# Two-layer hybrid mixer on one core: pacing of the second norm, both first weight splits in one projection job, and scan projections by segments

## Chip, cores and metric

One core of one Trainium2 chip. The metric is the device time of one execution in microseconds (us), the median of several runs. All inputs and outputs are float32; the projections run on TensorE (PE in the rows) as three passes of rounded parts, as told below.

## What is computed

Two layers over 512 latent tokens and 256 context tokens of width 1024. Each layer normalises the tokens, projects them (`w_in`), runs three mixers beside one another (windowed attention, a gated linear scan called GLA, a retention scan), merges them, projects again (`w_out`), adds the result to the stream, normalises a second time and runs a gated MLP with a width-3 convolution, whose down projection is added to the stream. The second layer computes the latent tokens alone from its queries on.

```python
h = rms_norm(x, norm1_g[l]) * (1.0 + sc1) + sh1
hc = rms_norm(ctx, norm1_g[l]) * (1.0 + csc1) + csh1
y, yc = token_mixers(h, hc, w_in[l], ...)
x = x + gt1 * y
h2 = rms_norm(x, norm2_g[l]) * (1.0 + sc2) + sh2
x = x + gt2 * conv_ffn(h2, ffn_up[l], ffn_conv_w[l], ffn_conv_b[l], ffn_down[l])
if with_ctx:
    ctx = ctx + cgt1 * yc
    ...

def rms_norm(a, g):
    af = a.astype(F32)
    y = af * lax.rsqrt(jnp.mean(af * af, axis=-1, keepdims=True) + EPS)
    return (y * g.astype(F32)).astype(a.dtype)
```

## The kernel before

Tokens lie along the free axis (768 columns: 512 latent, 256 context), channels on the partitions, 8 blocks of 128. A projection is a list of **jobs** (`Job`), one per 128 output channels. A job multiplies its weights with the 8 blocks k of the input; each block takes three passes, because weights and input are split into a high part and a remainder: high by high (`hh,wh`), low by high (`hl,wh`), high by low (`hh,wl`). `chunk` (L460) issues the three passes of one block for each segment of columns it is given; a segment has 512 or 256 columns and takes one matmul per pass. The result stands in one of two PSUM buffers `pg`, so a job's first matmul waits until the job before the previous one has been evacuated.

`flow` (L489) writes all jobs out in one order by hand; there is no scheduler. For job n it issues the split of the next job's weights (`split_w`, L433: ScalarE, ACT in the rows, writes `wh`; VectorE, DVE, writes `wl`, or GpSimd, POOL, where `job.pool` is set), the evacuation of the job before, and loads by SyncE (SP) two jobs ahead. With `by_seg` false a job runs block after block and both segments of each; with `by_seg` true it runs all 8 blocks of the first segment and then all 8 of the second (L551). `eager` (L565) lists extra calls after the second block.

Side work (attention, scans, rows of adaLN) is cut into steps; `beat` (L376) is called after each pass and lets steps follow at a rate per microsecond of matmul work. While a norm is under way its steps go first, at the rate `FRONT` (L191), by the norm's width.

`Norm` is the part that the change is about. `square` (L233) adds up the squares of a residual block as it is made; after the eighth it defers, by `wait` us of matmul work, the sums on PE (L252), the square root on ACT (L255), the reciprocal on DVE (L257), for some norms an ACT table load (L259), and later the transposes on PE (L277). `steps` (L269) then makes, for block k+1, the scaled block `h` or `room` (DVE, L288), its high part `hh` (ACT, L290) and, if the block's number is odd, the shifted block (ACT, L292); and for block k the low part `hl`, on DVE where k is even (L309), on POOL where k is odd (L307). In the projections L288 writes into four slots `room` in turn, so block 7 needs what block 3 has left.

Three places in the program have a norm between two projections: **boundary 1** (layer 0: `w_out`, then the MLP's up projection), **boundary 2** (layer 0's last part of the down projection, then the first jobs of layer 1) and **boundary 3** (layer 1: `w_out`, then up). At each, `ordered` (L572) gives twelve jobs: four over both segments, four over the first segment, then four over the second segment alone, which reuse the weights of the four before. In boundaries 1 and 2 the segments have 512 and 256 columns, in boundary 3 256 and 256. I call the last four jobs 9 to 12. While they run, the first segment's norm is under way on DVE, ACT and POOL, and each job's residual (X, L1325, DVE) frees its PSUM buffer. Then come two jobs together, a and b (`flow`, the tuple case), which start on the first segment as its blocks appear: a0, a1, a2, b0, a3, b1, a4, b2 and so on, three passes each. Their `wl` is made by POOL. The eager list of jobs 9 to 12 is: load a's weights, load b's weights, split a's, split b's.

Of the kernel before, what the change touches and what calls it, by code (L numbers as in the profile page):

```python
# [187 lines left out]
RATE = [(1.198, 2.0, 0.693, 0.817), (1.26, 1.65, 0.655, 1.08)]  # L188

LAG = [{'add': 2.4, 'parts': 0.4, 'low': 1.8, 'newton': 1.6, 'rs': 4.2, 'keys': 10.4, 'hi2': 5.0, 'lo2': 1.5}, {'add': 3.6, 'parts': 0.2, 'low': 0.8, 'newton': 1.6, 'rs': 2.2, 'keys': 6.8, 'hi2': 4.2, 'lo2': 2.3}]  # L190
FRONT = {256: 1.0, 512: 0.7}  # L191


class Job:
# [120 lines left out]
class Prog:  # L315
# [60 lines left out]
    def beat(self, us):  # L376
        self.age(us)
        self.due += us * (FRONT[self.front[0].b - self.front[0].a] if self.front else self.rate)
        while self.due >= 1.0:
# [554 lines left out]
    def gla_jobs(self, l, nq):  # L934
        nc = self.nc
        A = [(0, 512), (512, 768)]
        qc = A if nq > 512 else A[:1]
        nqc = qc[-1][1]
        T = {}

        def pre():
            self.gla = T
            T["qk"] = self.slot(4, [128, 2, 2, TA], name="gqk")
            T["v"] = self.slot(3, [128, 6, 512], name="gv")

            T["ga"] = self.cp.tile([98, TA], F32R, name="ga", tag="ga", bufs=1)
            nc.scalar.activation(out=T["ga"][96:98, :], in_=self.c("ones", 0, 1)[96:98].to_broadcast([2, TA]), func=AF.Copy)
            if l == 0:
                ts = self.t2("ts", (128, 256))
                nc.sync.dma_start(out=ts, in_=self.i["con"][:, CON["tsf"][0]:])  # L950
                self.defer(6.0, lambda: nc.scalar.activation(out=self.ts, in_=ts, func=AF.Copy))
            raw = self.t2("gw", (98, 512))
            nc.sync.dma_start(out=raw, in_=self.i["gw"][l])
            gw = T["gw"] = self.cp.tile([98, 512], F32R, name="gw", tag="gd", bufs=1)

            def parts():
                nc.scalar.activation(out=gw, in_=raw, func=AF.Copy)
                self.defer(1.5, lambda: nc.vector.tensor_tensor(out=gw[64:97], in0=raw[64:97], in1=gw[64:97].bitcast(F32), op=ALU.subtract))

            self.defer(6.0, parts)  # L960

        def ev_ga(ps):
            ga = T["ga"]
            low = self.t3("galow")[0:32]
            nc.scalar.activation(out=low, in_=ps[32:64, 0:TA], func=AF.Copy)
            nc.vector.tensor_tensor(out=low, in0=ps[0:32, 0:TA], in1=low, op=ALU.add)

            def parts():
                for n in (0, 64):
                    nc.scalar.activation(out=ga[n:n + 32], in_=low, func=AF.Copy)  # L970
                self.defer(1.5, lambda: nc.vector.tensor_tensor(out=ga[32:64], in0=low, in1=ga[0:32].bitcast(F32), op=ALU.subtract))

            self.defer(1.5, parts)

        jobs = [Job(self.i["wga"][l], self.h, A, ev_ga, m=32, pre=pre)]
        for p in range(2):
            jobs.append(self.win(l, U_GK + p, A, lambda ps, p=p: nc.scalar.activation(
                out=T["qk"][:, 1, p, :], in_=ps[:, 0:TA], func=AF.Copy)))
        jobs += self.value_jobs(l, 0, lambda: T["v"])
        for p in range(2):  # L980
            jobs.append(self.win(l, U_GQ + p, qc, lambda ps, p=p: nc.scalar.activation(
                out=T["qk"][:, 0, p, 0:nqc], in_=ps[:, 0:nqc], func=AF.Copy, scale=0.125)))
        return jobs

    def gla_mix(self, l, nq):
# [140 lines left out]
    def ret_jobs(self, l, nq):  # L1126
        nc = self.nc
        A = [(0, 512), (512, 768)]
        qc = A if nq > 512 else A[:1]
        T = {}  # L1130

        def start():

            self.need(f"att1{l}")
            self.ret = T
            T["qk"] = self.slot(0, [128, 2, 2, TA], name="rqk")
            T["v"] = self.slot(1, [128, 6, 512], name="rv")

        def ev(which, p, cols, sc):
            def f(ps):  # L1140
                n = cols[-1][1]
                dst = T["qk"][:, which, p, :]
                nc.scalar.activation(out=dst[:, 0:n], in_=ps[:, 0:n], func=AF.Copy, scale=sc)
                self.defer(1, lambda: self.rope(dst[:, 0:TL], dst[:, 0:TL]))
            return f

        def values():
            if not T:
                start()
            return T["v"]  # L1150

        jobs = self.value_jobs(l, 1, values)
        for which, u0, cols, sc in ((1, U_RK, A, 0.125), (0, U_RQ, qc, 1.0)):
            for p in range(2):
                jobs.append(self.win(l, u0 + p, cols, ev(which, p, cols, sc)))
        return jobs

    def ret_tables(self, l):
# [169 lines left out]
    def layer_jobs(self, l):  # L1328
# [6 lines left out]
        big = not last  # L1335
        mod = self.mod[l]
        jobs = []
# [80 lines left out]
        norm2 = [Norm(self, self.X, "n2g", l, 24, 32, [seg], tag="sc2" if l == 0 else None) for seg in segs]  # L1418
# [23 lines left out]
        def xin(n):  # L1442
            if n < len(order):
                d, sg = order[n]
                t = o["xin"][n] = self.t3("xin")
                lo, hi = sg[0][0], sg[-1][1]
                nc.sync.dma_start(out=t[:, lo:hi], in_=self.xd[:, d, lo:hi])

        def ev_o(n):
            d, sg = order[n]  # L1450

            def f(ps):
                self.residual(self.X, d, o["xin"].pop(n), ps, lambda d, v: o["g1"][:, d, v:v + 1], sg)
                xin(n + 2)
                for nm in norm2:
                    if nm.segs[0] in sg:

                        nm.square(d, 4.8 if big and nm is norm2[1] else 1.6)
            return f

        def away(k):
# [110 lines left out]
    def ordered(self, order, evac, src, h, nk, homes):  # L1572


        jobs, by = [], {}
        for n, (d, segs) in enumerate(order):
            cols = [(0, 512)] if segs == [(0, 256), (256, 512)] else segs
            jobs.append(Job(src(d), h, cols, evac(n), nk=nk, share=by.get(d)))
            by.setdefault(d, jobs[-1])
            jobs[-1].home = homes.get(d)  # L1580
        for n, (f, d) in enumerate(((Prog.load, 4), (Prog.load, 4), (Prog.split_w, 2), (Prog.split_w, 2))):
            jobs[n - 4].eager = [(f, d)]
        return jobs

    def X(self, k):
# [142 lines left out]
```

## Time and profile before

| | |
|---|---|
| median of 3 runs | 2336.31 us (2336.05 to 2337.02) |
| the profiled execution's own time | 2335.84 us |
| its span | 2334.0 us |
| PE busy | 2296.7 us (98%), 13610 matmuls and as many weight loads |
| DVE, ACT, POOL busy | 1416.2, 930.1, 298.8 us (61%, 40%, 13%) |
| mean granted PE clock | 0.998 of full speed |
| HBM traffic | 100 GB/s over the span, DMA queues busy 31% |

A row of the timeline gives start, length, engine, line, operation, what it writes and reads, shape and count, and in brackets the engine's idle time before it with what ended it. Matmuls overlap in the pipeline, so their rate is read from the distance of their starts, not from their length.

### The profile page before, as it was taken

What the parts mean: (1) busy time and instruction counts of PE and PEld (TensorE: products, weight loads), DVE (VectorE), ACT (ScalarE), POOL (GpSimd) and SP (SyncE); (2) the same over time, 40 slices, a digit from 0 to 9 for tenths busy, and PEclk for the clock granted to TensorE, in tenths of its full rate; (3) what the DMA queues carried; (4) which work ended last, traced back from release to release, by engine and by line L of the source; (5) the groups of instructions that cost most, each with busy time, mean ns of one, the idle gap of its engine ahead of it and who ended that gap; (6) DMA issues with size and microseconds to landing.
All of it is one profiled execution on the core that took longest, in us unless ns stands there. A gap on an engine that the chain in (4) does not pass through costs nothing.

```text
span 2334.0 us, 35318 instructions
## 1 busy us (share of the span) xinstructions
PE 2296.7 (98%) x13610; PEld 1987.5 (85%) x13610; DVE 1416.2 (61%) x2856; ACT 930.1 (40%) x1623; POOL 298.8 (13%) x256
## 2 busy tenths in 40 slices
PE   8999999999999999999999999999999999999999
PEld 6888888888888888888888887989888888888887
DVE  5756475523778477866786656546753555646564
ACT  5655533322322253313323346554443335434342
POOL 0211164000111020000000024113500211000000
PEclk9999999999999999999999999999999999999999
DMA  7111112222444333453363322111233233332333
GB/s 269 49 40 41 49 55 95 91 67 84 147 163 147 104 100 118 131 181 95 103 195 95 102 84 71 45 46 51 95 115 116 95 108 105 100 100 91 99 100 100
DMA packets 132840, 235.79 MB, mean 101 GB/s; under 512 B 14460, under 2 KB 25980, under 8 KB 132544
## 3 DMA queue, kind: packets, MB, share of 16 engines
q1 hardware_dynamic: 123200, 223.57, 29.8%
q10 hardware_dynamic: 9472, 9.96, 1.2%
q8 instruction: 107, 1.75, 0.3%
q14 instruction: 61, 0.50, 0.1%
HBM read 220.37 MB, written 13.11 MB: 100 GB/s over the span
## 4 chain that ended last, share of the span: by engine, by line
PE 58%; DVE 2%; ACT 2%; POOL 1%; issue 1%; DMA 0%; POOLq 0%; ACTq 0%; DVEq 0%
PE pg L473 51%; PE pg L485 3%; PE pm L912 1%; PE pm L901 1%; PE pm L1093 0%; PE ps L848 0%; PE ps L849 0%; POOL hl L307 0%; DVE wl L457 0%; PE pm L1115 0%; POOL at L1082 0%; ACT wh L455 0%; DVE qs L1056 0%; PE pm L1116 0%; DVE Sr L1106 0%
## 5 line engine op out<-in xcount | busy, mean ns | idle before, releaser
L473 PE MATMUL pg<-hh,wh 128*128 128x512 f32 (+1 forms) x2384 | 816.6, 354 | 9.1 <-DVE X L1325 3.6
L473 PE MATMUL pg<-hl,wh 128*128 128x512 f32 (+1 forms) x2384 | 814.7, 354 | 0.8 <-POOL hl L307 0.7
L473 PE MATMUL pg<-hh,wl 128*128 128x512 f32 (+1 forms) x2384 | 812.4, 353 | 1.0 <-DVE wl L457 0.7
L457 DVE TENSOR_TENSOR wl<-raw,wh 128x512 fp32r<-128x512 f32 x500 | 356.7, 722 | 340.3 <-ACT wh L455 295.4
L473 PEld LDWEIGHTS pg<-hh,wh 128*128 128x128 f32 x2384 | 439.2, 190 | 75.4 <-issue 5.0
L473 PEld LDWEIGHTS pg<-hl,wh 128*128 128x128 f32 x2384 | 439.8, 190 | 60.9 <-POOL hl L307 1.3
L473 PEld LDWEIGHTS pg<-hh,wl 128*128 128x128 f32 x2384 | 439.3, 190 | 61.1 <-issue 1.3
L455 ACT ACTIVATE wh<-raw 128x512 fp32r<-128x512 f32 (+1 forms) x556 | 334.6, 618 | 322.0 <-PE pg L473 176.5
L656 DVE SCALAR_TENSOR_TENSOR junk<-adr,crow 128x512 f32<-128x512 f32 x256 | 193.7, 757 | 15.0 <-DMA adr<-adv 7.1
L457 POOL TENSOR_TENSOR wl<-raw,wh 128x512 fp32r<-128x512 f32 x56 | 75.8, 1367 | 757.6 <-PE pg L473 544.2
L473 PE MATMUL pg<-al,wh 128*128 128x512 f32 (+1 forms) x500 | 171.4, 357 | 0.5 <-DVE al L576 0.5
L473 PE MATMUL pg<-ah,wh 128*128 128x512 f32 (+1 forms) x500 | 170.9, 356 | 0.0
L473 PE MATMUL pg<-ah,wl 128*128 128x512 f32 (+1 forms) x500 | 170.5, 355 | 0.0
L1313 POOL TENSOR_TENSOR M<-M,sg 128x768 f32<-128x768 f32 (+1 forms) x30 | 58.3, 1943 | 533.6 <-DVE sg L1311 533.6
L1301 ACT ACTIVATE sg<-pg 128x768 f32<-128x768 f32 (+1 forms) x48 | 33.7, 702 | 216.4 <-PE pg L473 216.4
L473 PEld LDWEIGHTS pg<-al,wh 128*128 128x128 f32 x500 | 91.4, 189 | 14.4 <-DVE al L576 1.1
L473 PEld LDWEIGHTS pg<-ah,wl 128*128 128x128 f32 x500 | 91.5, 189 | 13.8
L473 PEld LDWEIGHTS pg<-ah,wh 128*128 128x128 f32 x500 | 91.2, 189 | 14.0 <-ACT ah L575 0.4
L1488 DVE SCALAR_TENSOR_TENSOR acc<-pg,sml,acc 128x511 f32<-128x511 f32 (+1 forms) x129 | 84.8, 657 | 28.6 <-ACT acc L1485 28.4
L1325 DVE SCALAR_TENSOR_TENSOR X<-pg,mod,X 128x512 f32<-128x512 f32 (+1 forms) x72 | 45.7, 659 | 87.6 <-PE pg L473 87.6
L1485 ACT ACTIVATE acc<-pg,sml 128x768 f32<-128x768 f32 (+1 forms) x86 | 75.5, 878 | 35.9 <-PE pg L473 35.3
L1490 DVE SCALAR_TENSOR_TENSOR acc<-pg,sml,acc 128x511 f32<-128x511 f32 (+1 forms) x129 | 85.3, 661 | 4.6
(282 smaller groups left out, 3096.6 us busy)
## 6 DMA issues: line engine op xcount, KB each, us to landing
raw<-win SPq DMA_DIRECT2D x184, 256.0 KB, 2.9
raw<-up SPq DMA_DIRECT2D x176, 256.0 KB, 2.9
adr<-adv SPq DMA_DIRECT2D x160, 256.0 KB, 3.3
raw<-dn SPq DMA_DIRECT2D x64, 256.0 KB, 2.8
raw<-wbr SPq DMA_DIRECT2D x48, 256.0 KB, 2.7
aw<-ada SPq DMA_DIRECT2D x32, 256.0 KB, 5.4
raw<-wv SPq DMA_DIRECT2D x32, 256.0 KB, 3.1
raw<-wo SPq DMA_DIRECT2D x32, 256.0 KB, 3.4
```

The source lines that it names most:

```text
L455: nc.scalar.activation(out=hi, in_=raw, func=AF.Copy)
L457: eng.tensor_tensor(out=lo, in0=raw, in1=hi.bitcast(F32), op=ALU.subtract)
L473: nc.tensor.matmul(job.ps[0:m, lo:hi], job.w[k // 4][a][:, k % 4, :], job.h(k, b)[:, lo:hi], start=(k == 0 and n == 0), stop=(k == job.nk ...
L485: nc.tensor.matmul(job.ps[:, 256 * t:256 * t + 256], job.h(k, b)[:, o:o + 128], job.w[k // 2][a][:, k % 2, :], start=(k == 0 and n == 0 an ...
L656: nc.vector.scalar_tensor_tensor(out=junk, in0=raw, scalar=1.0, in1=cr[v], op0=ALU.mult, op1=ALU.mult, accum_out=acc)
L901: nc.tensor.transpose(pt[:, n * 128:n * 128 + 128], pr[n][:, b * 128:b * 128 + 128], self.c("ident"))
L1301: nc.scalar.activation(out=sgs[d][:, 0:n], in_=ps[:, 0:n], func=AF.Tanh, scale=0.5)
L1313: eng.tensor_tensor(out=m, in0=m, in1=sg[:, 0:n], op=ALU.add)
L1325: nc.vector.scalar_tensor_tensor(out=X(d)[:, lo:hi], in0=ps[:, lo:hi], scalar=gate(d, int(lo >= TL)), in1=xin[:, lo:hi], op0=ALU.mult, op1 ...
L1485: nc.scalar.activation(out=acc[:, 0:nq], in_=ps[:, 0:nq], func=AF.Identity, scale=cw(1), bias=self.s("cb", 44 * l + u))
L1488: nc.vector.scalar_tensor_tensor(out=acc[:, lo + 1:hi], in0=ps[:, lo:hi - 1], scalar=cw(0), in1=acc[:, lo + 1:hi], op0=ALU.mult, op1=ALU.add)
L1490: nc.vector.scalar_tensor_tensor(out=acc[:, lo:hi - 1], in0=ps[:, lo + 1:hi], scalar=cw(2), in1=acc[:, lo:hi - 1], op0=ALU.mult, op1=ALU.add)
```

## The change

`FRONT` goes from 1.0 to 0.9 for norms of 256 columns and from 0.7 to 0.48 for those of 512. The second segment's norm in boundary 1 starts its sums after 3.2 instead of 4.8 us of matmul work. Job 11 of each boundary splits both a's and b's weights; job 12 splits none. GLA's key and query jobs, retention's key and query jobs, and jobs 2 to 4 of each boundary run by segments; where such a job has one segment only (the queries of layer 1, and boundary 3) nothing changes by that.

```diff
-FRONT = {256: 1.0, 512: 0.7}
+FRONT = {256: 0.9, 512: 0.48}
@@ gla_jobs
+        for j in jobs[1:3] + jobs[-2:]:
+            j.by_seg = True
         return jobs
@@ ret_jobs
                 jobs.append(self.win(l, u0 + p, cols, ev(which, p, cols, sc)))
+                jobs[-1].by_seg = True
@@ layer_jobs, ev_o
-                        nm.square(d, 4.8 if big and nm is norm2[1] else 1.6)
+                        nm.square(d, 3.2 if big and nm is norm2[1] else 1.6)
@@ ordered
             jobs[-1].home = homes.get(d)
-        for n, (f, d) in enumerate(((Prog.load, 4), (Prog.load, 4), (Prog.split_w, 2), (Prog.split_w, 2))):
-            jobs[n - 4].eager = [(f, d)]
+            jobs[-1].by_seg = n in (1, 2, 3)
+        jobs[-4].eager = jobs[-3].eager = [(Prog.load, 4)]
+        jobs[-2].eager = [(Prog.split_w, 2), (Prog.split_w, 3)]
         return jobs
```

No instruction is added or removed: each engine has as many as before, in another order. Four lines are added, so L1325 is L1328 in the changed kernel.

POOL, boundaries 1 and 2, before (`wl`: low part of weights of a and b; `hl`: low part of an odd block of the norm, `room` in boundary 1 and `h` in boundary 2):

```order
L307 TENSOR_TENSOR hl<-room,hh 128x512
L457 TENSOR_TENSOR wl<-raw,wh 128x512 x2
L307 TENSOR_TENSOR hl<-room,hh 128x512
L457 TENSOR_TENSOR wl<-raw,wh 128x512 x2
L307 TENSOR_TENSOR hl<-room,hh 128x512 x2
L307 TENSOR_TENSOR hl<-room,hh 128x256 x4
L457 TENSOR_TENSOR wl<-raw,wh 128x512 x2
L307 TENSOR_TENSOR hl<-h,hh 128x512
L457 TENSOR_TENSOR wl<-raw,wh 128x512 x2
L307 TENSOR_TENSOR hl<-h,hh 128x512 x3
```

The same in the changed kernel:

```order
L307 TENSOR_TENSOR hl<-room,hh 128x512
L457 TENSOR_TENSOR wl<-raw,wh 128x512 x4
L307 TENSOR_TENSOR hl<-room,hh 128x512 x3
L307 TENSOR_TENSOR hl<-room,hh 128x256 x4
L457 TENSOR_TENSOR wl<-raw,wh 128x512 x4
L307 TENSOR_TENSOR hl<-h,hh 128x512 x4
```

All four `wl` now stand together: ahead of block 3's `hl` in boundary 1, ahead of block 1's in boundary 2. In boundary 3, where one pair of `wl` stood ahead of the `hl` of block 3 and the other behind that of block 5, the four stand ahead of block 3's too.

DVE, boundary 2, before, from the second residual of the second segment on (X: residual, sq: running sum of squares, h: scaled block):

```order
L1325 SCALAR_TENSOR_TENSOR X_7380<-pg,mod_107,X_7380 128x256
L244 TENSOR_TENSOR sq<-sq 128x256
L288 SCALAR_TENSOR_TENSOR h<-X_7379,A,ps 128x512 x2
L309 SCALAR_TENSOR_TENSOR hl<-h,mod_108,hh 128x512
L1325 SCALAR_TENSOR_TENSOR X_7380<-pg,mod_107,X_7380 128x256
L244 TENSOR_TENSOR sq<-sq 128x256
L288 SCALAR_TENSOR_TENSOR h<-X_7380,A,ps 128x512
L1325 SCALAR_TENSOR_TENSOR X_7380<-pg,mod_107,X_7380 128x256
```

The same in the changed kernel:

```order
L1328 SCALAR_TENSOR_TENSOR X_7380<-pg,mod_107,X_7380 128x256
L244 TENSOR_TENSOR sq<-sq 128x256
L288 SCALAR_TENSOR_TENSOR h<-X_7379,A,ps 128x512
L1328 SCALAR_TENSOR_TENSOR X_7380<-pg,mod_107,X_7380 128x256
L244 TENSOR_TENSOR sq<-sq 128x256
L288 SCALAR_TENSOR_TENSOR h<-X_7379,A,ps 128x512
L309 SCALAR_TENSOR_TENSOR hl<-h,mod_108,hh 128x512
L1328 SCALAR_TENSOR_TENSOR X_7380<-pg,mod_107,X_7380 128x256
```

Job 11's residual moves ahead of block 3 and of block 2's `hl`; job 12's keeps the same work before it but one block. In boundary 1 job 11's residual passes one block, job 12's two more and block 4's `hl`.

DVE, boundary 3, before, from job 10's residual to job 12's (X_18192 holds blocks 0 to 3, X_18193 blocks 4 to 7):

```order
L1325 SCALAR_TENSOR_TENSOR X_18193<-pg,g_18190,xin 128x256
L244 TENSOR_TENSOR sq<-sq 128x256
L288 SCALAR_TENSOR_TENSOR room<-X_18193,A,ps 128x256 x2
L309 SCALAR_TENSOR_TENSOR hl<-room,mod_108,hh 128x256
L1325 SCALAR_TENSOR_TENSOR X_18193<-pg,g_18190,xin 128x256
L244 TENSOR_TENSOR sq<-sq 128x256
L288 SCALAR_TENSOR_TENSOR room<-X_18193,A,ps 128x256 x2
L309 SCALAR_TENSOR_TENSOR hl<-room,mod_108,hh 128x256
L1325 SCALAR_TENSOR_TENSOR X_18193<-pg,g_18190,xin 128x256
```

The same in the changed kernel:

```order
L1328 SCALAR_TENSOR_TENSOR X_18193<-pg,g_18190,xin 128x256
L244 TENSOR_TENSOR sq<-sq 128x256
L288 SCALAR_TENSOR_TENSOR room<-X_18192,A,ps 128x256
L309 SCALAR_TENSOR_TENSOR hl<-room,mod_108,hh 128x256
L288 SCALAR_TENSOR_TENSOR room<-X_18193,A,ps 128x256 x2
L309 SCALAR_TENSOR_TENSOR hl<-room,mod_108,hh 128x256
L1328 SCALAR_TENSOR_TENSOR X_18193<-pg,g_18190,xin 128x256
L244 TENSOR_TENSOR sq<-sq 128x256
L288 SCALAR_TENSOR_TENSOR room<-X_18193,A,ps 128x256 x2
L309 SCALAR_TENSOR_TENSOR hl<-room,mod_108,hh 128x256
L1328 SCALAR_TENSOR_TENSOR X_18193<-pg,g_18190,xin 128x256
```

Job 10's residual passes block 3 and block 2's `hl`. Between it and job 11's stand now blocks 3, 4 and 5 with two `hl`, and between that and job 12's, as before, blocks 6 and 7 with block 6's `hl`.

ACT there, before, from block 3's shifted copy on (wh: high part of weights):

```order
L292 ACTIVATE room<-room,mod_108 128x256
L239 ACTIVATE sq<-X_18193 128x256
L455 ACTIVATE wh<-raw 128x512 x2
L290 ACTIVATE hh<-room,mod_108 128x256 x2
L292 ACTIVATE room<-room,mod_108 128x256
L239 ACTIVATE sq<-X_18193 128x256
L290 ACTIVATE hh<-room,mod_108 128x256
L455 ACTIVATE wh<-raw 128x512 x2
```

The same in the changed kernel, from the square of job 10's residual on:

```order
L239 ACTIVATE sq<-X_18193 128x256
L290 ACTIVATE hh<-room,mod_108 128x256
L292 ACTIVATE room<-room,mod_108 128x256
L455 ACTIVATE wh<-raw 128x512 x4
L290 ACTIVATE hh<-room,mod_108 128x256 x2
L292 ACTIVATE room<-room,mod_108 128x256
L239 ACTIVATE sq<-X_18193 128x256
L290 ACTIVATE hh<-room,mod_108 128x256 x2
```

Block 3's `hh` and shifted copy moved behind that square, and the four `wh` follow them without a break, ahead of block 4's `hh`.

## Rows read from the trace of the kernel before

**Rows 1.** The page, busy time of the engines.

```profile
PE 2296.7 (98%) x13610; PEld 1987.5 (85%) x13610; DVE 1416.2 (61%) x2856; ACT 930.1 (40%) x1623; POOL 298.8 (13%) x256
```

**Rows 2.** Who waited for whom, PE alone: us in total, times, longest.

```profile
PE pg L473 <- DVE X L1325: 3.6, 3, 2.1
...
PE ps L1070 <- DVE qs L1056: 1.8, 3, 1.1
```

**Rows 3.** PE by stretches: four jobs block by block, then four by segments (matmuls).

```profile
753.28:787.20 33.92, 33.92 (x194) 1.00 0.43 136
854.42:887.78 33.36, 33.36 (x194) 1.00 0.35 111
```

**Rows 4.** Stretches after waits at boundaries 1, 2, 3; granted clock is third from the end.

```profile
827.50:832.40 4.90, 4.88 (x14) 3.85 (x15) 1.75 (x2) 1.99 (x4) 2.48 (x2) 0.65 0.51 176
1384.10:1390.00 5.90, 4.95 (x25) 3.92 (x26) 3.81 (x6) 5.32 (x9) 5.59 (x5) 1.00 0.68 222
...
1968.30:1971.70 3.40, 3.40 (x19) 3.40 (x18) 1.32 (x4) 1.88 (x4) 0.00 (x0) 0.50 0.02 5
```

**Rows 5.** Timeline of PE, boundary 1: a0, b0, and the third job's fifth block.

```profile
823.14 0.47 PE L473 MATMUL pg<-hh,wh 128*128 128x512 f32 x1 [0.27 <-DVE X L1325]
...
827.52 0.47 PE L473 MATMUL pg<-hh,wh 128*128 128x512 f32 x1 [2.08 <-DVE X L1325]
...
849.15 0.50 PE L473 MATMUL pg<-hh,wl 128*128 128x512 f32 x1 [0.68 <-DVE wl L457]
```

**Rows 6.** Timeline of POOL, then DVE, boundary 1.

```profile
820.10 3.00 POOL L457 TENSOR_TENSOR wl<-raw,wh 128x512 fp32r<-128x512 f32 x2 [0.32 <-ACT wh L455]
823.06 1.28 POOL L307 TENSOR_TENSOR hl<-room,hh 128x512 fp32r<-128x512 f32 x1
824.31 3.14 POOL L457 TENSOR_TENSOR wl<-raw,wh 128x512 fp32r<-128x512 f32 x2
...
825.21 1.11 DVE L309 SCALAR_TENSOR_TENSOR hl<-room,mod,hh 128x512 fp32r<-128x512 f32 x1
...
826.90 0.47 DVE L1325 SCALAR_TENSOR_TENSOR X<-pg,g,xin 128x256 f32<-128x256 f32 x1
```

**Rows 7.** Timeline of PE, then POOL and DVE, boundary 2.

```profile
1384.16 0.47 PE L473 MATMUL pg<-hh,wh 128*128 128x512 f32 x1 [1.23 <-DVE X L1325]
...
1386.81 0.83 PE L252 MATMUL pm<-con,sq 128*128 128x2 f32 x6 [0.47 <-ACT sq L239]
...
1389.33 0.50 PE L473 MATMUL pg<-hl,wh 128*128 128x512 f32 x1 [0.42 <-POOL hl L307]
...
1380.51 2.56 POOL L457 TENSOR_TENSOR wl<-raw,wh 128x512 fp32r<-128x512 f32 x2 [538.18 <-PE pg L473]
1383.02 1.74 POOL L307 TENSOR_TENSOR hl<-h,hh 128x512 fp32r<-128x512 f32 x1
...
1381.76 1.85 DVE L309 SCALAR_TENSOR_TENSOR hl<-h,mod,hh 128x512 fp32r<-128x512 f32 x1
```

**Rows 8.** Timeline of PE, POOL, DVE and ACT, boundary 3.

```profile
1965.37 0.36 PE L473 MATMUL pg<-hh,wh 128*128 128x256 f32 x1 [1.40 <-ACT wh L455]
...
1966.11 0.39 PE L473 MATMUL pg<-hh,wl 128*128 128x256 f32 x1 [0.28 <-POOL wl L457]
...
1960.24 2.73 POOL L457 TENSOR_TENSOR wl<-raw,wh 128x512 fp32r<-128x512 f32 x2 [1.73 <-ACT wh L455]
1962.93 1.61 POOL L307 TENSOR_TENSOR hl<-room,hh 128x256 fp32r<-128x256 f32 x2
1964.78 2.51 POOL L457 TENSOR_TENSOR wl<-raw,wh 128x512 fp32r<-128x512 f32 x2 [0.24 <-ACT wh L455]
...
1963.89 0.48 DVE L288 SCALAR_TENSOR_TENSOR room<-X,A,ps 128x256 f32<-128x256 f32 x1 [0.24 <-POOL hl L307]
...
1964.75 0.47 DVE L1325 SCALAR_TENSOR_TENSOR X<-pg,g,xin 128x256 f32<-128x256 f32 x1
...
1959.55 1.14 ACT L455 ACTIVATE wh<-raw 128x512 fp32r<-128x512 f32 x2
```

## Prediction

> **What bounds the kernel now.** I read the page first: PE is busy for 2296.7 us, 98% of the span [rows 1], so all that this change can win is some 37 us of waits and whatever makes PE's own stream quicker. The list of who waited for whom says where the waits are: the largest between projections is for the residual X, 3.6 us in three waits; the scans have some of their own, as 1.8 us for `qs` [rows 2]. Then the timeline at the three boundaries. At boundary 1, PE waits 0.27 us before a and 2.08 before b, each for X, and later 0.68 for a `wl` [rows 5]; at boundary 2, 1.23, 0.47 and 0.42 [rows 7]; at boundary 3, 1.40 and 0.28 [rows 8]. Last the granted clock by stretches: 0.65 in the 4.90 us after boundary 1's long wait, with 14 matmuls, and 0.50 in 3.40 us soon after boundary 3's; at boundary 2 it stayed at 1.00 [rows 4]. 0.50 is the lower of PE's two levels, 1.2 of 2.4 GHz. So a wait here can cost more than its length.
>
> **Projections by segments.** Four jobs block by block take 33.92 us, four by segments 33.36, with the same matmuls [rows 3]: 0.14 us a job. By segments a pair of a 512 and a 256 takes 33.36 / 96 = 0.35 us, by columns 0.23 and 0.12, which I use below. PE has as many weight loads as matmuls [rows 1], so segments add no load. Twelve scan jobs have two segments and change (eight in layer 0, the four key jobs in layer 1), three in layer 0's `w_out`, three in its last down projection with 21 pairs instead of 24: 12 x 0.14 + 3 x 0.14 + 3 x 0.12 = **-2.5 us**. The last six, 0.8 us, run alone as the jobs of the rows do. Among the scans' steps the gain may shrink to nothing, and the steps themselves fall in other places against PE: the `qs` waits show that a few tenths either way are in reach there, and I keep 1.5 us to both sides.
>
> **Boundary 1.** What goes: the two waits for X, 0.27 + 2.08; its 14 matmuls at full speed are 14 x 0.23 = 3.2 us, so the slow stretch cost 4.90 - 3.2 = 1.7 [rows 4]; and the 0.68 for `wl`, since two rows of adaLN that stood before that split on DVE now come later. Together 4.7. SP issues four loads of up weights ahead of two `crow` loads and the first adaLN rows for the same reason; those feed layer 0's last gate and layer 1, and the two parts of the MLP in between cover them.
>
> What comes: job 11's residual passes one block, so a starts at 822.87, where PE is free (823.14 less 0.27). Job 12's residual passes block 4's `hl` and two blocks; `hl` and one block are 1.69 us by the starts at 825.21 and 826.90 [rows 6]. But ACT has two more `wh` to do ahead of the square of job 11's residual, and so it comes at 825.2 and not at 824.6: b waits some 0.9 us for it. Next is POOL: its four `wl` start at 820.10 as before and now run without a break, 3.00 + 3.14, to 826.2; block 3's `hl` takes 1.28 and is there at 827.5, where it was at 824.3 [rows 6]. PE wants it for the fourteenth matmul, 822.87 + 13 x 0.23 = 825.85. So the new waits are 1.65 us in two pieces, whichever part b takes. Whether the clock falls after them no row shows: three pieces of 2.12 at boundary 2 left it alone, 2.35 in two pieces here did not [rows 4, 5, 7]. I take no fall, as the nearest row in pieces. Sum 1.65 - 4.7 = **-3.1 us**, between -4.1 (POOL at its unhindered 1.28 an operation, 0.65 of wait) and -1.4 (the clock falls).
>
> The Trainium skill, "TensorE: Matmul & The Clock Gate", section "What's actually happening", says that the slow clock is the default and that activity releases it. The fall after 2.35 us of waits and none after 2.12 agree with a watch over recent activity and leave open what 1.65 does; by that rule the sum here could as well be -1.4.
>
> **Boundary 2.** The three waits, 2.12 us, lose their cause: job 11's residual now comes before block 3 and block 2's `hl`, of which that `hl` alone took 1.85 [rows 7], so a starts when PE is free, 1384.16 - 1.23 = 1382.93. But POOL does four `wl` before block 1's `hl`, where it did two. They start at 1380.51; the first two take 2.56 [rows 7], the next two as much or 3.14 [rows 6], so `hl` begins at 1385.6 to 1386.2 and, with 1.28 [rows 6] to 1.74 [rows 7], ends at 1386.9 to 1387.9; I take 1387.4. PE wants it for its fifth matmul, 1382.93 + 4 x 0.23 = 1383.85, and waits **3.55 us**, longer in one piece than any wait in the rows. After 2.35 and 1.68 the clock fell, so I add one slow stretch of 1.7. What is late next is hidden by it: the sums, the square root and the table load now stand ahead of blocks 4 to 7 on ACT and DVE, which would cost a further 1 us at full speed. Sum -2.12 + 3.55 + 1.7 = **+3.1 us**; ends +0.9 (early `hl`, no fall) and +4.6 (late `hl`, the fall, and that 1 us on top).
>
> Why 1.28 and 1.74: the longer one ran beside DVE's `hl` of 1.85, which it held up in turn [rows 7]. The Trainium skill, "SBUF — State Buffer", section "Who interferes with whom", says that a VectorE instruction with two inputs in SBUF and a GpSimd instruction that reads SBUF wait for one another in full. The rows agree in kind. By that rule every `wl` that meets a DVE subtraction is the long one, and the sum is the upper, +3.6.
>
> **Boundary 3.** Here the chain runs through three engines. Before, `wh` started on ACT at 1959.55 and POOL at 1960.24 [rows 8]. Now job 10's residual comes 1.1 us sooner, but block 3's `hh` and shifted copy (0.5 each) stand ahead of the `wh`, which start at about 1960.3, and POOL at 1961.0. First effect: four `wh` take 4 x 0.55 (1.14 a pair [rows 8]), to 1962.5; then block 4's `hh`, its `hl` and only then job 11's residual, 0.5 + 0.6 + 0.47: 1964.05. a was due at 1962.9 (b's 1965.37 less its wait of 1.40 and nine matmuls of 0.12) and starts at 1964.2: 1.3 us. Second: POOL's four `wl`, 2.73 + 2.51 [rows 8], end at 1966.2, block 3's `hl` (half of 1.61) at 1967.0. Block 7 needs the slot that this frees: the wait of 0.24 "<-POOL hl" shows it [rows 8]. From the start of that block to the end of job 12's residual took 1964.75 + 0.47 - 1963.89 = 1.33, so b starts at about 1968.5; it is due nine matmuls of 0.12 after a, 1965.3: **3.2 us**. Against 1.40 + 0.28 before: **+2.8 us**. The slow stretch is there in both. Ends: +1.4 if POOL and ACT are a microsecond earlier than I have them, +4.3 if two slow stretches follow: the second costs 3.40 less the 16 matmuls of 0.12 in it [rows 4], about 1.5.
>
> **Sum.** -2.5 - 3.1 + 3.1 + 2.8 = +0.3 us on the profiled execution's 2335.84, so 2336.1; it lies 0.47 below the median, 2336.31, which gives **2336.6 us**. From 0.2% on (4.7 us) a measurement can tell such a kernel from no change, so I forecast none.
>
> **Rivals.** First, faster: the waits go and nothing takes their place, because ACT and POOL get through their pairs before PE asks. Then the boundaries give -4.7, -2.1 and -3.2 (1.68 and the slow stretch's 1.5), with the segments -12.5: 2323.8, and about 2330 if half holds. For it speaks that the DVE order does put the residuals sooner; against it that POOL's 1.28 an operation and its start leave block 1's `hl` at boundary 2 three us late even unhindered. Chance 0.16.
>
> Second, the scans: steps in the by-segment jobs follow one another more evenly, and 3 us of their waits go: 2334. The rows show the waits [rows 2], not their cure. 0.08.
>
> Third, slower: the clock. Each of the longer waits is followed by a slow stretch, boundary 1's too (+1.7), boundary 3's by two (+1.5), and boundary 2 stands at its upper end (+1.5): 4.7 above the forecast, **2341.3 us**. It decides by the granted clock: from the first stretch at 0.50 behind boundary 1's b on. For it speaks that 4.5 us of waits fall in six at boundary 3; against it that 2.12 left no trace at boundary 2. 0.14.
>
> Fourth, the segments do not do what they did alone, since the scans' steps stand between the matmuls: -0.8 instead of -2.5, 2338.3. 0.12.
>
> **Chances.** Forecast 0.50, rivals 0.16, 0.08, 0.14, 0.12. Faster by over 0.2%: the first rival and a hundredth, 0.17. Slower by over 0.2%: the third and a hundredth, 0.15. Within 0.2%: 0.68. The range that leaves out most of the first rival and half of the third is 2331.6 to 2341.0.
>
> **What would show it.** In the changed kernel's timeline at boundary 2, a's fifth matmul with 3 to 4 us of idle before it, ended by POOL's `hl` (L307), and 0.50 of clock soon after. At boundary 3, about 1.3 us before a and 3 before b, both ended by X (L1328). At boundary 1, no wait before a, under 2 us in all up to the fourteenth matmul, ended by `hl` on POOL, the clock at 1.00, and no wait at the third job. Jobs 2 to 4 of `w_out` at 8.34 us each. I am wrong if POOL's `hl` ends no long wait at boundary 2, or if the segmented scan jobs gain or lose more than 2 us.

## The result and the profile after

The changed kernel takes **2348.84 us** (median of 6 runs, 2348.01 to 2352.86), the kernel before 2336.51 in the runs beside it: ratio 1.0057, interval 1.0044 to 1.0070. It is slower by 12.3 us, outside the range and with the sign to which I gave 0.15. The profiled execution took 2348.73 us with a span of 2346.9, against 2334.0.

PE's busy time grew by 6.2 us with as many instructions, so part of the loss isn't waiting; the waits for X (3.6 us before [rows 2]) and for POOL's `hl` (0.7) grew. The page of the changed kernel, busy time of the engines [answers to rows 1]:

```profile
PE 2302.9 (98%) x13610; PEld 1990.9 (85%) x13610; DVE 1416.9 (60%) x2856; ACT 930.0 (40%) x1623; POOL 297.2 (13%) x256
```

and who waited for whom, PE alone: us in total, times, longest [answers to rows 2]. First `hl` in the kernel before, then the changed kernel:

```profile
PE pg L473 <- POOL hl L307: 0.7, 2, 0.4
...
PE pg L473 <- DVE X L1328: 5.3, 3, 2.9
PE pg L473 <- POOL hl L307: 4.5, 4, 3.6
```

To find the place I cut both traces at the same matmuls: each stretch below begins and ends with the same job in both. Columns: window, its length, busy time and instructions of PE, PEld, DVE, ACT, POOL, granted clock, DMA share, GB/s. The kernel before; the five rows are layer 0 up to job 12 of `w_out`, boundary 1 (that job and the pair), boundary 2 (the last down job and layer 1's first pair), layer 1's scans, boundary 3:

```profile
20.31:819.83 799.52, 787.73 (x5193) 688.58 (x5194) 475.46 (x1042) 315.99 (x578) 139.87 (x116) 1.00 0.29 94
819.83:845.02 25.19, 22.84 (x133) 19.78 (x131) 16.38 (x31) 17.79 (x33) 12.84 (x11) 0.93 0.34 102
...
1380.24:1404.18 23.94, 21.19 (x129) 18.39 (x128) 15.66 (x27) 17.98 (x33) 15.20 (x13) 1.00 0.31 102
1404.18:1695.32 291.14, 283.60 (x2081) 249.15 (x2081) 177.35 (x400) 154.25 (x302) 93.24 (x84) 1.00 0.19 60
...
1959.85:1980.66 20.81, 18.25 (x133) 17.27 (x131) 10.68 (x25) 13.90 (x29) 10.43 (x11) 0.92 0.22 64
```

The changed kernel, the same five:

```profile
20.72:818.24 797.52, 785.36 (x5192) 686.59 (x5193) 475.86 (x1042) 315.63 (x578) 139.34 (x116) 1.00 0.29 94
818.24:841.62 23.38, 21.74 (x132) 18.46 (x131) 15.64 (x27) 16.63 (x31) 12.53 (x11) 1.00 0.21 63
...
1376.47:1406.15 29.68, 25.36 (x129) 21.45 (x127) 13.96 (x27) 17.91 (x33) 14.90 (x13) 0.83 0.26 88
1406.15:1703.48 297.33, 287.14 (x2080) 250.41 (x2081) 178.55 (x400) 154.52 (x302) 92.77 (x84) 0.99 0.18 59
...
1967.98:1993.53 25.55, 20.04 (x132) 18.86 (x131) 10.51 (x24) 14.78 (x31) 10.40 (x11) 0.87 0.19 52
```

Layer 0 gained 2.0, boundary 1 1.8, the MLP between 0.4; boundary 2 lost 5.7, **layer 1's scans 6.2**, boundary 3 4.7. That makes +12.5 before rounding; the start, 0.4 later, brings it to the 12.9 between the spans. The boundaries have the signs that I forecast. The scans, which I had put at nought, are the largest term.

Layer 0's gain isn't the segments' alone. Before had this stretch there, with PE busy throughout at the lower clock, so up to half of it, 1.7 us, is the clock's; the changed kernel has none in layer 0:

```profile
29.54:32.95 3.41, 3.41 (x24) 2.12 (x16) 2.49 (x7) 1.91 (x4) 0.06 (x1) 0.50 1.06 384
```

The waits forecast at the boundaries are there. Boundary 2 in the changed kernel, timeline of POOL and of PE, then the stretch with the clock at its lower level:

```profile
1376.73 5.65 POOL L457 TENSOR_TENSOR wl<-raw,wh 128x512 fp32r<-128x512 f32 x4 [536.58 <-PE pg L473]
1382.35 2.49 POOL L307 TENSOR_TENSOR hl<-h,hh 128x512 fp32r<-128x512 f32 x2
...
1383.66 0.80 PE L473 MATMUL pg<-hl,wh 128*128 128x512 f32 x1 [3.57 <-POOL hl L307]
...
1382.61:1392.85 10.24, 9.19 (x27) 7.50 (x28) 3.13 (x6) 3.71 (x6) 2.23 (x2) 0.50 0.27 85
```

Four `wl` and only then block 1's `hl`; a's fifth matmul waits 3.57 us. Then 9.19 us of PE's work ran at 0.50, which is half of it lost, 4.6 us. Boundary 3, timeline of PE (a0, b0) and the stretch at the lower level there:

```profile
1972.54 0.36 PE L473 MATMUL pg<-hh,wh 128*128 128x256 f32 x1 [1.52 <-DVE X L1328]
...
1976.74 0.55 PE L473 MATMUL pg<-hh,wh 128*128 128x256 f32 x1 [2.89 <-DVE X L1328]
...
1976.53:1983.36 6.83, 6.62 (x31) 6.65 (x32) 0.56 (x4) 2.15 (x4) 0.73 (x1) 0.50 0.01 2
```

Boundary 1, PE: b0, a later block of each segment, the third job.

```profile
824.24 0.47 PE L473 MATMUL pg<-hh,wh 128*128 128x512 f32 x1 [0.89 <-DVE X L1328]
...
832.49 0.50 PE L473 MATMUL pg<-hl,wh 128*128 128x512 f32 x1 [0.16 <-POOL hl L307]
...
840.21 0.39 PE L473 MATMUL pg<-hl,wh 128*128 128x256 f32 x1 [0.51 <-POOL hl L307]
...
845.77 0.50 PE L473 MATMUL pg<-hh,wl 128*128 128x512 f32 x1 [0.68 <-DVE wl L457]
```

### The profile page after: what moved, and what is told of

The parts are those of the page before. It is cut to its first block, busy times and chain, and to the rows that moved or that the text cites. A ratio compares the mean times of both kernels' runs of the same rounds, so it can differ in the third digit from the quotient of the medians.

```text
span 2346.9 us, 35310 instructions
## 1 busy us (share of the span) xinstructions
PE 2302.9 (98%) x13610; PEld 1990.9 (85%) x13610; DVE 1416.9 (60%) x2856; ACT 930.0 (40%) x1623; POOL 297.2 (13%) x256
## 4 chain that ended last, share of the span: by engine, by line
PE 57%; DVE 2%; issue 2%; ACT 2%; POOL 1%; DMA 0%; POOLq 0%; ACTq 0%; DVEq 0%
PE pg L473 50%; PE pg L485 3%; PE pm L912 1%; PE pm L901 1%; PE pm L1095 0%; POOL wl L457 0%; PE ps L848 0%; POOL hl L307 0%; DVE wl L457 0%; PE ps L849 0%; PE pm L1117 0%; PE pm L1118 0%; ACT wh L455 0%; DVE qs L1058 0%; ACT QS L737 0%
## 5 line engine op out<-in xcount | busy, mean ns | idle before, releaser
L473 PE MATMUL pg<-hh,wh 128*128 128x512 f32 (+1 forms) x2384 | 836.5, 355 | 9.5 <-DVE X L1328 5.3
L473 PE MATMUL pg<-hl,wh 128*128 128x512 f32 (+1 forms) x2384 | 835.2, 354 | 4.9 <-POOL hl L307 4.5
L473 PE MATMUL pg<-hh,wl 128*128 128x512 f32 (+1 forms) x2384 | 832.8, 353 | 0.7 <-DVE wl L457 0.7
L473 PEld LDWEIGHTS pg<-hh,wh 128*128 128x128 f32 x2384 | 449.0, 190 | 73.8 <-issue 5.0
L473 PEld LDWEIGHTS pg<-hl,wh 128*128 128x128 f32 x2384 | 449.0, 190 | 67.0 <-POOL hl L307 7.1
L473 PEld LDWEIGHTS pg<-hh,wl 128*128 128x128 f32 x2384 | 448.7, 190 | 60.1 <-issue 1.7
L1328 DVE SCALAR_TENSOR_TENSOR X<-pg,mod,X 128x512 f32<-128x512 f32 (+1 forms) x72 | 45.8, 659 | 86.8 <-PE pg L473 86.8
```

Source lines behind the costliest of these rows:

```text
L473: nc.tensor.matmul(job.ps[0:m, lo:hi], job.w[k // 4][a][:, k % 4, :], job.h(k, b)[:, lo:hi], start=(k == 0 and n == 0), stop=(k == job.nk ...
L1328: nc.vector.scalar_tensor_tensor(out=X(d)[:, lo:hi], in0=ps[:, lo:hi], scalar=gate(d, int(lo >= TL)), in1=xin[:, lo:hi], op0=ALU.mult, op1 ...
```

## The experiments

Theory A: the joint split of a's and b's weights, by putting POOL's four `wl` ahead of `hl`, makes the losses at boundaries 2 and 3. Rivals: the slower norm pace makes them (B), or layer 1's loss follows from the way boundary 2 ends (C) or from the segmented key jobs (D). All kernels were timed in 5 rounds; where before is named, it ran beside them.

### One part alone, or one part undone

**Everything but the joint split** (e1), against the change:

```diff
-        jobs[-4].eager = jobs[-3].eager = [(Prog.load, 4)]
-        jobs[-2].eager = [(Prog.split_w, 2), (Prog.split_w, 3)]
+        for n, (f, d) in enumerate(((Prog.load, 4), (Prog.load, 4), (Prog.split_w, 2), (Prog.split_w, 2))):
+            jobs[n - 4].eager = [(f, d)]
```

> The changed kernel with the old eager list: job 11 splits a's weights, job 12 splits b's. Theory A (the joint split puts POOL's four wl ahead of block 1's and block 3's hl; the long waits at boundaries 2 and 3 and the slow clock behind them come from that): no wait of 3.6 us at boundary 2, no two stretches at 0.50 at boundary 3, and 10.5 us (5.75 + 4.74 of the job-by-job difference) come back: about 2338.3 us, still above before by what layer 1's scans lose. Rival B (the slower pace of the norm does it): the waits stay, 2348. Rival C (layer 1's scans lose their 6.2 us because boundary 2 ends in another place and clock): these come back too, 2332.

**The joint split alone** (e2): before with the two lines marked - above in place of the two marked +.

> Before with the joint split of a's and b's weights in job 11 alone. Theory A: the long wait for POOL's hl at boundary 2 with a long stretch at 0.50 behind it, and about 3 us before b at boundary 3 (X); layer 1's scans as before: +5.75 + 4.74, less what boundary 1 gives, 2346. Rival B (pace): as before, 2336.5, with waits below 2 us at both places. Rival C: layer 1's scans lose 6 us as well, 2352.

**The scans' segments alone** (e3), against before:

```diff
+        for j in jobs[1:3] + jobs[-2:]:
+            j.by_seg = True
...
+                jobs[-1].by_seg = True
```

> Before with the scans' key and query jobs by segments alone. Theory D (the segmented key jobs of layer 1 make scan steps late, and PE waits for them): layer 0 -1.3 us, layer 1 +6.2, so 2341.4, with the waits of 0.84 at the second GLA key job, 1.69 at the second gate job and so on. Prediction's step: 8 x 0.14 less and no waits, 2335. Rival C (the losses in layer 1 follow from the state in which boundary 2 leaves the kernel): 2335 too, without the new waits in layer 1.

**The pace alone** (e4), against before:

```diff
-FRONT = {256: 1.0, 512: 0.7}
+FRONT = {256: 0.9, 512: 0.48}
...
-                        nm.square(d, 4.8 if big and nm is norm2[1] else 1.6)
+                        nm.square(d, 3.2 if big and nm is norm2[1] else 1.6)
```

> Before with the slower pace of the norms and the earlier sums of boundary 1 alone. Theory A: boundary 1 loses its waits (-1.8 us), boundaries 2 and 3 within 1 us of before, the rest as before: 2334.7. Rival B (the pace makes the long waits): +10.5 at boundaries 2 and 3, 2345. If layer 1's 6.2 us come from the pace, they show here: 2341.

Measured, with before at 2335.53: e1 **2342.31** (ratio 1.0030, 1.0019 to 1.0041), e2 **2345.28** (1.0047, 1.0033 to 1.0061), e3 **2334.75** (0.9996, 0.9987 to 1.0004), e4 **2345.48** (1.0045, 1.0032 to 1.0058). The same cuts in each trace, lengths in us (s is layer 1's scans; they end at the first matmul of the merge's branches):

```
          bound. 1   bound. 2   s        bound. 3
before    25.19      23.94      291.14   20.81
change    23.38      29.68      297.33   25.55
e1        26.16      24.93      295.69   21.65
e2        25.13      28.16      291.09   24.79
e3        23.62      23.93      291.08   20.04
e4        26.21      25.42      298.41   21.87
```

D falls: with the segments alone the scans take 291.08 us, as before. C falls: in e2 boundary 2 ends late and the scans take 291.09. A holds for boundaries 2 and 3: the joint split alone costs 4.2 and 4.0 us there, the pace alone 1.5 and 1.1. What I had given to no theory in this size is **the pace: it carries the loss in layer 1**, 7.3 us in e4 and 4.6 in e1, though no norm is under way in these scans. So e4 missed its 2334.7. What e1 missed its 2338.3 by lies elsewhere: of the 10.5 us, boundaries 2 and 3 gave back 8.6, and boundary 1 took 2.8 more than in the change. There the pace with the old eager list makes PE wait 1.80 us for POOL's `hl`, in e1 and in e4, and in both 6.83 us at 0.50 follow.

### A counter that is carried over

`beat` adds pace times matmul work to `due`, and each whole 1.0 in it lets one step go. Norm steps and side steps share `due`, and it isn't set back when a norm ends. Counted through the program, what is left after layer 1's first pair is 0.433 before, in e2 and in e3, and 0.614 in the changed kernel, e1 and e4: the kernels with 291 us and those with more. So the theory, E: the pace shifts each of layer 1's scan steps by a fraction of a step, up to one pass of a chunk. Set by hand (e5, against before; e6 has the same line with 0.43304, against the change):

```diff
                 prev = b
+                if norms is self.norm1[1]:
+                    self.due = 0.61424
```

> Before, with one number set by hand: after layer 1's first pair the counter `due`, which says when the next side step may be issued, is set to 0.614 instead of the 0.433 that is left there. 0.614 is what the slower norm pace leaves. Pace, joint split and segments are as before. Theory E (layer 1's scans lose because each of their steps is issued up to one pass of a chunk earlier): layer 1 loses 5 to 7 us between its first pair and its merge, with the waits of 0.84 for P, 1.69 for ke and so on; boundaries as before: 2341.5 us. Rival F (the loss comes from what the norm and the splits do to DVE and ACT, not from the place of the steps): within 1 us of before, 2335.5.

> The changed kernel with `due` set to 0.433 after layer 1's first pair, as it stood before the change. Theory E: layer 1's 6.2 us come back, the boundaries stay as in the changed kernel: 2342.6 us. Rival F: 2348.8.

Measured: e5 **2343.26** (2338.91 to 2346.08), ratio to before (2336.35) 1.0034, 1.0021 to 1.0046; e6 **2344.29** (1.0036, 1.0023 to 1.0049), 4.6 less than the change. Layer 1's scans in e5:

```profile
1402.24:1699.19 296.95, 285.65 (x2081) 249.48 (x2081) 176.56 (x400) 154.82 (x302) 92.99 (x84) 1.00 0.18 60
```

and in e6:

```profile
1407.89:1698.98 291.09, 283.66 (x2081) 248.92 (x2081) 177.22 (x400) 154.47 (x302) 94.15 (x84) 1.00 0.18 60
```

One number, which adds no work, makes the loss or takes it away. How it does is seen in GLA's first key job of layer 1. Timeline of PE before:

```profile
1446.65 0.88 PE L901 MATMUL pm<-con,P 128*128 128x128 f32 x4
1447.28 0.60 PE L473 MATMUL pg<-hh,wh 128*128 128x512 f32 x2
1447.72 0.51 PE L473 MATMUL pg<-hl,wh 128*128 128x512 f32 x2
1448.07 0.60 PE L901 MATMUL pm<-con,P 128*128 128x128 f32 x4
1448.42 0.60 PE L473 MATMUL pg<-hh,wl 128*128 128x512 f32 x2
1448.86 0.51 PE L473 MATMUL pg<-hh,wh 128*128 128x512 f32 x2
1450.55 0.44 PE L848 MATMUL ps<-KK,QS 128*128 128x384 f32 x1 [1.18 <-DVE st L860]
```

and in e5 (two lines added, so L901 is L903):

```profile
1445.73 1.32 PE L903 MATMUL pm<-con,P 128*128 128x128 f32 x4 [0.82 <-DVE P L896]
1446.81 0.60 PE L473 MATMUL pg<-hh,wh 128*128 128x512 f32 x2
1447.25 0.60 PE L903 MATMUL pm<-con,P 128*128 128x128 f32 x4
1447.60 0.60 PE L473 MATMUL pg<-hl,wh 128*128 128x512 f32 x2
1448.03 0.51 PE L473 MATMUL pg<-hh,wl 128*128 128x512 f32 x2
1450.70 0.44 PE L850 MATMUL ps<-KK,QS 128*128 128x384 f32 x1 [2.15 <-DVE st L862]
```

The second group of `P` (attention weights) and the first `ps` stand one pass earlier in PE's stream, and there are 0.82 and 2.15 us of waits instead of 1.18. But the first of them is before a group that stands where it stood, and PE comes to it as long after the start of the scans as before, 42.5 us. It is DVE that is late, because its steps have changed places too. DVE before (`qraw`: queries being rotated, `st`: sums of the softmax), then in e5:

```profile
1442.61 0.68 DVE L673 TENSOR_TENSOR qraw<-rt,sw 128x512 f32<-128x512 f32 x1
1444.11 0.16 DVE L887 TENSOR_TENSOR st<-st 128x4 f32<-128x4 f32 x1
1445.43 1.61 DVE L894 TENSOR_SCALAR P<-P,st 128x512 f32<-128x512 f32 x3
...
1442.19 0.16 DVE L889 TENSOR_TENSOR st<-st 128x4 f32<-128x4 f32 x1 [1.41 <-ACT st L876]
1443.51 1.10 DVE L675 TENSOR_TENSOR qraw<-rt,sw 128x512 f32<-128x512 f32 x1
1445.20 1.27 DVE L896 TENSOR_SCALAR P<-P,st 128x512 f32<-128x512 f32 x3
```

Before, DVE rotates the queries while ACT makes `st`. In e5 the step with `st` stands ahead of that, DVE stands idle for 1.41 us, and `P` is begun 42.96 us after the start of the scans instead of 41.25. The changed kernel has the same 1.41. The end of the rotation is a call deferred by matmul work, which `due` doesn't move; the steps of the attention go by `due`, so their order changes.

The changed kernel has waits of 0.84 and 1.30 in PE's rows there, and 1.69 for `ke` (keys of the retention scan) where before had 0.55. By the rows of the scans PE's idle time (length less busy time) grew from 7.5 us to 11.3 in e5 and to 10.2 in the change. In the change the clock adds up to 1.7 us, half of this stretch:

```profile
1693.22:1696.63 3.41, 3.41 (x18) 3.19 (x18) 0.63 (x1) 0.00 (x0) 0.00 (x0) 0.50 0.23 75
```

The rest, 2.05 us in e5 and 1.8 in the change, is longer busy time with as many matmuls, which I haven't taken apart.

### The remaining parts, and what is left without them

**All segments of the change, on before** (e7):

```diff
+        for j in jobs[1:3] + jobs[-2:]:
+            j.by_seg = True
...
+                jobs[-1].by_seg = True
...
+            jobs[-1].by_seg = n in (1, 2, 3)
```

> Before with all the segments of the change (scans' key and query jobs, jobs 2 to 4 of each boundary), but neither the slower pace nor the joint split. The prediction's step: the scans' segments measured 0.8 us, jobs 2 to 4 of w_out and of the last down projection add 3 x 0.14 + 3 x 0.12: 2334.75 - 0.8 = 2334.0 us. Rival: the moved evacuations and norm steps of jobs 2 to 4 cost as much at the boundaries: 2335.

Measured: **2334.11**, ratio 0.9993, 0.9984 to 1.0002: 2.2 us less than before, near the -2.5 of the prediction, but not told apart from nothing, nor from the rival's 2335.

**The counter moved to the other side** (e8): e7 with `self.due = 0.25` in the place shown.

> The same with `due` set to 0.25 after layer 1's first pair, so that its steps are issued up to one pass later than before. Theory E in its simple form (earlier steps wait for DVE, later ones don't): the waits for st, lgp, ab and ke in layer 1 shrink by up to 2 us: 2332 us. Rival (the steps' places decide case by case, and the table of lags was made for the old places): 2 to 5 us slower, 2337.

Measured: **2338.15** (1.0010, 1.0001 to 1.0019), 4.0 above e7, and the scans take 294.89 us; up to 1.7 of the 3.7 above e7's 291.15 is the clock's, which stood at 0.50 for 3.41 us from 1688.30 on. That earlier is worse and later better is refuted: both shifts lose, as the rival said; whether the lags were made for the old places wasn't tested.

**The change with the old eager list and the old counter** (e9): e1 and the 0.43304 together.

> The changed kernel with the old eager list and with `due` at 0.433 after layer 1's first pair: two of its three losses undone, the pace and the segments left. If joint split and carried counter are the whole loss: the 2342.3 us measured with the old list, less the 5.0 that layer 1's scans lost in that trace: 2337.3 us, the rest above before being some 1 us at each boundary. Rival (part of the loss is neither): 2340 or more.

Measured: **2339.80** (1.0010, 1.0001 to 1.0018), 2.5 above the forecast and 0.2 short of the rival's. Its eleven runs fall into three at 2335.1 to 2335.5, with a mean clock of 0.998 to 0.999, and eight at 2339.4 to 2341.4, with 0.994 to 0.996. The profiled execution is one of the three: scans 291.11 us, boundaries 23.99, 25.29 and 22.67. PE's idle time at the three boundaries is 7.5 us in all there and 8.0 in e7's profile, so the order of the instructions adds no waiting in sum. What the pace still costs goes with the clock, as far as this trace shows: it stood at 0.50 for 3.41 us at boundary 2 and for 6.83 at boundary 3, in e7's for 3.41 at boundary 1 alone. Where it falls in the eight no trace shows.

**Boundary 1's part alone** (e10): e7, with the joint split, the pace and the earlier sums for that boundary only, and the counter set at the first job of the last down projection to where e7 has it (`joint` is given for that boundary alone).

```diff
+SLOW = {256: 0.9, 512: 0.48}
...
-        self.due += us * (FRONT[self.front[0].b - self.front[0].a] if self.front else self.rate)
+        self.due += us * ((SLOW if getattr(self.front[0], 'slow', False) else FRONT)[self.front[0].b - self.front[0].a] if self.front else self.rate)
...
+                nm.slow = big
...
-                        nm.square(d, 4.8 if big and nm is norm2[1] else 1.6)
+                        nm.square(d, 3.2 if big and nm is norm2[1] else 1.6)
...
+                jobs[-len(order)].pre = lambda: setattr(self, "due", 0.7233)
...
+        if joint:
+            jobs[-2].eager = [(Prog.split_w, 2), (Prog.split_w, 3)]
+            jobs[-1].eager = []
```

> Before with all segments, and with the joint split, the slower pace and the earlier sums in boundary 1 alone; `due` is set at the first job of the last down projection so that boundaries 2, 3 and layer 1's scans run as before. Theory: boundary 1 gains the 1.8 us that it gained in the changed kernel, on top of the 2334.1 measured with the segments: 2332.3 us, with 0.9 us of wait before b for X and no slow clock there. Rival (boundary 1's gain was the absence of a slow stretch by chance): 2334.

Measured: **2334.15** (0.9992, 0.9983 to 1.0001), as e7 and as the rival said. Boundary 1 has the forecast 0.89 us of wait before b and takes 23.40 us, 1.8 less than in e7's profile, and yet the median shows no gain. In the profile boundary 3, whose order is e7's, loses as much: 21.89 us with a stretch at 0.50, against 20.07 without one. Such stretches come and go at boundary 1 too. e3 has boundary 1 in before's order; PE's timeline there, and the stretch behind the wait:

```profile
827.71 0.47 PE L473 MATMUL pg<-hh,wh 128*128 128x512 f32 x1 [2.08 <-DVE X L1328]
...
831.00 0.95 PE L252 MATMUL pm<-con,sq 128*128 128x2 f32 x8
...
827.71:832.60 4.89, 4.89 (x25) 4.16 (x26) 1.96 (x4) 2.56 (x6) 2.47 (x2) 1.00 0.48 179
```

The same wait of 2.08 us, and the clock stays at 1.00: the 14 matmuls ahead of the sums (L252) take 3.29 us where before's took 4.90 [rows 4]. (The row's 25 are these, the eight small sums and three more.) Boundary 1 takes 23.62 us. Of the five profiles with before's order at boundary 1 three have the slow stretch (before, e7, e8) and two haven't (e3, e5); of the four with the change's order (the change, e6, e10, e12) none has. So 0.2 us of the gain is there without the clock, 23.62 to 23.40, and 1.6 hang on a stretch that comes and goes between executions. Whether the change makes it rarer these nine don't settle.

**Boundary 2 alone undone** (e12): the change with the old eager list in the last down projection.

> The changed kernel with the old eager list in the last down projection (boundary 2) alone. Theory A: boundary 2 loses the wait of 3.57 us for POOL's hl and most of the slow clock behind it, 5.75 - 1.0 = 4.75 us; the rest stays: 2344.1 us, with waits under 0.7 us at boundary 2. Rival (the slow clock follows whatever waits are there, in pieces too): about 2346.

Measured: **2343.00** (1.0032, 1.0021 to 1.0044), 5.8 less than the change; 4.75 was forecast. Boundary 2 in e12, timeline of POOL, then PE, then the whole:

```profile
1376.58 2.56 POOL L457 TENSOR_TENSOR wl<-raw,wh 128x512 fp32r<-128x512 f32 x2 [536.62 <-PE pg L473]
1379.09 1.46 POOL L307 TENSOR_TENSOR hl<-h,hh 128x512 fp32r<-128x512 f32 x1
1380.51 2.97 POOL L457 TENSOR_TENSOR wl<-raw,wh 128x512 fp32r<-128x512 f32 x2
...
1380.61 0.50 PE L473 MATMUL pg<-hl,wh 128*128 128x512 f32 x1 [0.68 <-POOL hl L307]
1384.78 0.51 PE L473 MATMUL pg<-hl,wh 128*128 128x512 f32 x1 [0.68 <-POOL hl L307]
...
1376.32:1401.22 24.90, 21.81 (x130) 18.09 (x128) 14.77 (x27) 18.00 (x33) 14.95 (x13) 1.00 0.30 106
```

Block 1's `hl` between the two pairs of `wl`: waits of 0.68 us, in all four of at most that, instead of one of 3.57, and the clock doesn't fall; 24.90 us instead of 29.68. Theory A is shown at this boundary in both directions, by e2 and by e12.

The medians, one change after the other: before 2336.35; with all segments 2334.11; and the pace, its counter put right, 2339.80; and the joint split 2344.29; and the counter as the pace leaves it 2348.84. They were timed beside runs of before with medians of 2336.35 to 2336.51. Neither e7 nor e10 is told apart from before.

## Why the prediction was wrong

**The step that failed most** is in the part on the segments: "the steps themselves fall in other places against PE ... I keep 1.5 us to both sides". I looked for such a shift in the segmented jobs alone, which moved nothing in layer 1's scans (291.08 us in e3), and bounded it by waits of before. The pace was costed only at the boundaries where norms run. That its remainder in `due` goes on into layer 1's scans I did not follow; measured, 4.6 to 6.9 us.

**Boundary 2** (+3.1 forecast, +5.7 measured). The wait was right: 3.55 forecast, 3.57 measured, by the right releaser. The term mis-sized is "I add one slow stretch of 1.7": the clock stood at 0.50 for 10.24 us, worth 4.6. With 3.57 less before's 2.12 of waits that is +6.0. The stretch isn't always so long. In e6 the same order has the wait of 3.58 and then this:

```profile
1385.33:1392.16 6.83, 6.76 (x21) 5.69 (x22) 0.81 (x2) 2.27 (x3) 1.25 (x2) 0.50 0.25 81
```

Two later waits of 0.39 and 0.61, which the longer stretch hides in the change, come out there, the "further 1 us at full speed" of the prediction, and the boundary takes the same 29.68. On POOL's rate, the upper end that I gave beside the Trainium skill's page "SBUF — State Buffer", section "Who interferes with whom", isn't borne out: the four `wl` took 5.65 us, 1.41 each, between the 1.28 of an unhindered operation and the 1.57 of the hindered pair (3.14 [rows 6]), while DVE's `hl` beside them took 1.11 us, not 1.85 [rows 7].

**Boundary 3** (+2.8, +4.7). The waits came within 0.3 us: 1.52 (1.3) and 2.89 (3.2). Mis-sized was "the slow stretch is there in both": behind the longer wait 6.62 us of work ran at 0.50 instead of 3.40 [rows 4], 1.6 us more of loss. All four profiles with the wait of 2.89 (the change, e2, e6, e12) have 6.83 us at 0.50 there; of six with before's order (before, e3, e5, e7, e8, e10) two have 3.41 and four none. This was rival three's second slow stretch, which I had priced at 1.5.

**Boundary 1** (-3.1, -1.8). Right: no wait before a, 0.89 before b (0.9), under 2 us in all, the clock at 1.00. The other piece, 0.75 for POOL's `hl` at the fourteenth matmul, was some 0.2, since the four `wl` took 5.67 us and not 6.14; that PE's idle time still comes to 1.64 (23.38 less 21.74), beside the forecast 1.65, is luck, for 0.16 and 0.51 of it are waits for later `hl`. Wrong: the 0.68 for `wl` at the third job, behind this stretch, is still there. Moving the adaLN rows behind that split did not free it, because DVE wasn't held up by them: ahead of the four convolution steps that come before the split it stood idle until ACT's `acc`, for 1.74 us before and for 4.00 in the change. And the slow stretch's 1.7 that I booked as won isn't shown to be the change's, as e3 and e10 tell. Of the rule that the slow clock is the default and activity releases it (the Trainium skill, "TensorE: Matmul & The Clock Gate", section "What's actually happening") these runs show both sides: after 1.64 us of waits in pieces no fall here, after one wait of 1.80 there in e4 (for POOL's `hl`) 6.83 us at 0.50. They show too that the fall isn't sure: after 1.83 there in e9, whose order at boundary 1 is e4's, none.

**Segments** (-2.5): -2.2 in the medians, inside the noise. Where the jobs run alone, the step held: `w_out`'s first four jobs take 33.50 us instead of 33.92 [rows 3], the segmented three 8.34 each, as forecast, and those of the last down projection 7.30 instead of 7.42.

```profile
752.12:785.62 33.50, 33.50 (x194) 29.51 (x193) 20.57 (x41) 8.36 (x16) 0.00 (x0) 1.00 0.43 139
```

Among the scans' steps 0.8 us was measured (e3) where 1.7 was forecast, inside the noise as well; rival four's -0.8 for all segments lies in e7's interval and stays open. Rival two found nothing. Of the rivals the third, slower by the clock, was nearest, but its 2341.3 held no loss in the scans. My range left out that a pace table has effects where it isn't read.

## What to carry to other kernels

Where steps are let go by a counter, look at what one stage leaves in it for the next: a change of pace moves every later step by a fraction, and here that cost 4.6 to 6.9 us, about as much as the 5.7 that the pace cost otherwise (e7 to e9). Set the counter at stage borders before pacing is compared, or each trial tests two things. And when work of two kinds shares an in-order engine, don't gather the kind that is needed last ahead of the one that the next engine waits for.

## What the runs showed of the hardware

The same instructions with the same wait of 2.08 us were followed by a fall of the clock in some executions (boundary 1 before, in e7 and e8) and by none in others (e3, e5). The waits of one order came out within 0.05 us of one another in these five; the falls did not. Longer single waits were mostly followed by more, but not always: 2.9 us at boundary 3 by 6.83 us at 0.50 (the change); 3.57 at boundary 2 by 10.24 there, and 3.58 in e6 by 6.83; 1.80 at boundary 1 by 6.83 in e1 and e4, and 1.83 in e9 by none. Short waits didn't always go free: four of 0.42 to 0.68 at boundary 2 in e12 were followed by none, two of 0.68 and 0.67 there in e9 by 3.41. So one long wait cost its length and up to 1.9 times that again (half of 6.83 for the 1.80 in e4; 4.6 for 3.57). And a fall seen in one profile is no property of the kernel: the executions of e9 with the lower mean clock took 4 to 6 us longer than the others.
